# The sample block moves from the last token group to the first, and block 7 takes its seat in the dense expert pass

## The chip, the cores and the metric

One core of a Trainium2 chip. The time is the device time of one execution in microseconds (us). The kernel before took 4423.67 us, the median of three runs (4419.91 to 4437.72).

## The reference, cut to what matters

One layer is run on 1024 prompt tokens and on 64 sample tokens (8 sequences of 8). Both share all weights.

```python
n = rmsnorm(x); z = n @ w_in              # 1024 -> 7192 columns, cut into q, k, v, gates of three branches
m = sigmoid(gate_0) * (gla(...) @ w_gla_o) + sigmoid(gate_1) * (fox(...) @ w_fox_o) \
    + sigmoid(gate_2) * (mem(...) @ w_mem_o)
h = x + m @ w_out
h = h + peer(rmsnorm(h))                  # per token: 8 heads x 16 experts out of 16384
y = rmsnorm(h)
```

GLA is linear attention with a running state, FoX is causal softmax attention with forget gates, mem attends to 256 memory tokens. For a prompt token FoX looks at the tokens before it in the prompt. A sample sequence looks at 1024 cached rows through a page table, has its own GLA state and its own memory cache. PEER scores 2 x 128 keys per head, takes the best 16 pairs, and for each of the 128 chosen experts of a token forms `gelu(x . u[e]) * g * v[e]`, summed. The tables `u` and `v` have 16384 rows of 1024 floats each.

## The kernel before

Tokens are handled in nine blocks: 0 to 7 are the prompt's (128 tokens each), block 8, called SAMPLE or S, is the 64 sample tokens. `GROUPS` (L42) puts them in three groups, and `base(grp)` (L636) runs everything up to the PEER scores for a group: all weights are streamed once per group, so a group of three blocks shares each weight load. A weight product goes through `mm_w` (L256), in two ways: with a block's activations stationary (256 columns wide for each block, S too), or with the weights stationary and the tokens of the group moving (`jobs_T`, 384 or 320 columns wide: a prompt block brings 128 tokens, S brings 64). Per group there are 512 matmuls of the second kind on each of three lines (L273, L274, L277).

For a prompt block `gla` (L389), `fox_prompt` (L550) and `mem_prompt_att` (L595) run per block. Block b's FoX covers b + 1 blocks of keys. For S, `fox_sample` (L1240) fetches the cached pages with indirect DMAs that GpSimd issues (L1237), transposes and multiplies them page by page, `mem_sample` (L1363) does the same with the memory caches, and `gla_sample` (L484) carries eight states.

PEER is done in two ways. The blocks that are not in `DENSE` are gathered: `peer_gather` (L1028) fetches, for each of a token's 128 experts, the row of `u` and the row of `v` with an indirect DMA on GpSimd (L1040, L1051), and VectorE does one dot product (L1042) and one multiply-add (L1057) on each fetched row of 128 x 1024. A block is 128 such u rows and 128 v rows. The rows pass through four buffers, five in the last stage. The blocks in `DENSE` (448 tokens) are multiplied with the whole of both tables on TensorE in `peer_dense` (L1122), after the last group; this needs a table of gate weights per expert and token, `c_scr`, which `expert_weights` (L1071) writes, 16 tokens at a time (a slab): 8 slabs for a prompt block, 4 for S.

`choose` (L919) picks the experts of a block. `LATER` names blocks whose top-16 search is put off into `choose`; `HERE` names the block whose top-16 stays on chip.

The order of the instructions on each engine is fixed by a scheduler from priorities, a lower number being more urgent. `base` has the most urgent ones. `at(None, ...)` places work at half a million and up, that is behind all of `base`; the gathers run from one million upwards (`prio`), so that they fill what `base` leaves free. The functions run in program order otherwise. `peer_dense` can begin only when `base` of the last group is done, since it takes over its memory (`early.close()`). In it, `expert_weights` of the dense block of the last group comes first (L1154 to L1156), then the expert loop; the first product with the gate weights (L1194) needs the whole first piece of `c_scr` (L1178).

So before: group 0 (blocks 0, 1, 2) alone; then group 1 (3, 4, 5) with the gathers of 0, 1, 2 in the background; then group 2 (S, 6, 7), with the same background and the expert weights of 3, 4, 5; then the dense pass of 3, 4, 5, S with the gathers of 6 and 7 beside it.

Of the kernel before, what the change touches and what calls it, by code (L numbers as in the profile page):

```python
# [38 lines left out]

ROWS, ROWS2 = 4, 5  # L40
SAMPLE = 8
GROUPS = [[0, 1, 2], [3, 4, 5], [SAMPLE, 6, 7]]  # L42

DENSE = [3, 4, 5, SAMPLE]

LATER = [6, 7]

HERE = [SAMPLE]
DG, DW = 8, 9
WR = 4  # L50
CB = {"hot": 4, "stg": 1, "eg": 1}
# [3 lines left out]
def tile_hybrid(ctx: ExitStack, tc: tile.TileContext, x_prompt, x_sample, cache_fox_k, cache_fox_v,  # L55
# [23 lines left out]
    def T(tag, shape, dt=F32):  # L79
        cnt[0] += 1  # L80
        return bp.tile(shape, dt, tag=tag, name=f"{tag}_{cnt[0]}", bufs=BUFS[tag])
# [16 lines left out]
    def evac(out, in_):  # L98
        A.activation(out, in_, AF.Copy)
# [522 lines left out]
    t_scr = [dp.tile([128, 512], F32, name=f"t_scr{b}") for b in range(9)]  # L622
    s_scr = {b: dp.tile([128, 2048], F32, name=f"s_scr{b}") for b in LATER}
    e_scr = {b: dp.tile([128, 128], I32, name=f"e_scr{b}") for b in DENSE}
    g_scr = {b: dp.tile([128, 128], F32, name=f"g_scr{b}") for b in DENSE}
    c_scr = dp.tile([sum(64 if b == SAMPLE else 128 for b in DENSE) // 16, 128, 2048], F32, name="c_scr")
    q_scr = dp.tile([128, 4, 64], F32, name="q_scr")
# [8 lines left out]
    def base(grp):  # L636
# [55 lines left out]
        for half in range(2):  # L692
# [55 lines left out]
            def fin_k(b, p):  # L748
# [11 lines left out]
                evac(kT[:, :, b * 128:(b + 1) * 128], pt[:, :256].rearrange("p (j t) -> p j t", t=128))  # L760
                if b < 7 and grp is not GROUPS[-1]:
                    SP.dma_start(kT_scr[half * 256:(half + 1) * 256, b * 128:(b + 1) * 128].rearrange(
# [118 lines left out]
        for hd in range(8):  # L881
# [5 lines left out]
            for b in grp:  # L887
# [5 lines left out]
                evac(s, p2[:, :256])  # L893
                if b in LATER:
                    SP.dma_start(s_scr[b][:, hd * 256:(hd + 1) * 256], s)
                    continue
                t = last_t[:, hd * 64:(hd + 1) * 64] if b in HERE else T("tp", [128, 64])
                top16(s, t)
                if b not in HERE:
                    SP.dma_start(t_scr[b][:, hd * 64:(hd + 1) * 64], t)  # L900

    def top16(s, t):

        for j in range(2):
            x, v = s[:, j * 128:(j + 1) * 128], t[:, j * 16:(j + 1) * 16]
            i = t[:, 32 + j * 16:48 + j * 16].bitcast(U32)
            V.max(v[:, 0:8], x)
            V.max_index(i[:, 0:8], v[:, 0:8], x)
            V.match_replace(x, v[:, 0:8], x, LOWEST)
            V.max(v[:, 8:16], x)  # L910
            V.max_index(i[:, 8:16], v[:, 8:16], x)
# [7 lines left out]
    def choose(b):  # L919

        if b not in DENSE:
            eidx[b] = gp.tile([128, 128], I32, tag="ei", name=f"ei{b}", bufs=2)
            gate_w[b] = gp.tile([128, 8, 16], F32, tag="gw", name=f"gw{b}", bufs=2)
        for hf in range(2):
            hs = slice(4 * hf, 4 * hf + 4)
            w = gp.tile([128, 864], F32, tag="ch", name=f"ch{b}_{hf}", bufs=1)
            t = w[:, 0:256].rearrange("p (h c) -> p h c", h=4)
            if b in LATER:
                for hd in range(4):
                    x = w[:, 352 + hd % 2 * 256:608 + hd % 2 * 256]  # L930
                    SP.dma_start(x, s_scr[b][:, (4 * hf + hd) * 256:(4 * hf + hd + 1) * 256])
                    top16(x, w[:, hd * 64:(hd + 1) * 64])
            elif b in HERE:
                t = last_t[:, hf * 256:(hf + 1) * 256].rearrange("p (h c) -> p h c", h=4)
# [6 lines left out]
            def region(o, n):  # L941
                return w[:, o:o + 4 * n].rearrange("p (h c) -> p h c", h=4)
# [34 lines left out]
            c = slice(hf * 64, (hf + 1) * 64)  # L977
            if b in DENSE:
                ei, gw = w[:, 528:592].bitcast(I32), region(656, 16)
# [13 lines left out]
            V.tensor_tensor(gw, gw, sm[:, :, None].to_broadcast([128, 4, 16]), op=OP.mult)  # L993
            if b in DENSE:
                SP.dma_start(e_scr[b][:, c], ei)
# [126 lines left out]
    def peer_dense(ctx2, dn):  # L1122
# [6 lines left out]
        def DT(tag, shape, dt=F32):  # L1129
            cnt[0] += 1  # L1130
            return dn.tile(shape, dt, tag=tag, name=f"d{tag}_{cnt[0]}", bufs=DB[tag])

        def DP(tag):
            cnt[0] += 1
            return pd.tile([128, 512], F32, tag=tag, name=f"p{tag}_{cnt[0]}", bufs=PB[tag])
# [18 lines left out]
        for b in DENSE:  # L1154
            if b in GROUPS[-1]:
                expert_weights(b, DT, lambda: DP("c"))  # L1156
# [16 lines left out]
        for g in range(128 // DG):  # L1173
            if g * DG % 8 == 0:
                c8 = DT("c", [128, NS, 128])
                ready = NS - sum(w for b, w in zip(DENSE, widths) if b in GROUPS[-1]) // 16
                for x in (slice(0, ready), slice(ready, NS)) if g == 0 else (slice(0, NS),):
# [239 lines left out]
    M = 10 ** 6  # L1417
    urgent = [M // 2]

    def at(prio, f, *args):  # L1420

        keep, tc.cur_priority = tc.cur_priority, prio or urgent[0]
        f(*args)
        if not prio:
            urgent[0] = tc.cur_priority
        tc.cur_priority = keep


    prio = [M]

    def gather(blocks):
        for i, b in enumerate(blocks):
            prio[0] += M
            if i + 1 < len(blocks):
                at(prio[0] + M // 2, choose, blocks[i + 1])
            at(prio[0], peer_gather, b)
        prio[0] += M

    for grp in GROUPS:
        pj3[0] = grp is GROUPS[0]  # L1440
        base(grp)
        mine = [b for b in grp if b not in DENSE]
        first = [b for b in grp if b in DENSE]
        if grp is not GROUPS[-1]:
            first = mine[:1] + first
        else:
            first += mine[:1]
        for b in first:
            if b in DENSE and grp is GROUPS[-1]:
                choose(b)  # L1450
            else:
                at(None, choose, b)
            if b in DENSE and grp is not GROUPS[-1]:
                at(None, expert_weights, b)
        if mine and grp is not GROUPS[-1]:
            gather(mine)
    early.close()
# [37 lines left out]
```

## Time and profile before

| | |
|---|---|
| median of three runs | 4423.67 us |
| the profiled execution | 4433.77 us, its span 4432.0 us |
| TensorE (PE) busy | 3755.6 us, 85% |
| VectorE (DVE) busy | 3346.1 us, 75% |
| ScalarE (ACT) busy | 1796.2 us, 41% |
| GpSimd (POOL) busy | 1679.1 us, 38% |
| mean granted TensorE clock | 0.890 of full speed |

Busy times of a stretch count every moment in which the engine had an instruction in flight. PEld is the weight load of TensorE. [...] "Idle before" in a group of instructions is the time that the engine waited just before them, with what ended the wait.

### The profile page before, as it was taken

How to read it: one execution, taken by the hardware profiler on the slowest of the kernel's cores; microseconds unless marked ns; L12 is line 12 of the kernel's file. 1: busy time of each engine (PE TensorE's matmuls, PEld its weight loads, DVE VectorE, ACT ScalarE, POOL GpSimd, SP SyncE). 2: the span in 40 equal slices, each digit the busy share in tenths (PEclk: the TensorE clock that was granted, in tenths of full speed). 3: DMA queues.
4: the chain of work that ended last, by engine and by line, in shares of the span. 5: the costliest groups of instructions: out<-in, count | busy, mean ns of one | idle time of the engine just before them, and what ended most of it. 6: DMA issues, size and time to landing. Idle time of an engine off the chain costs nothing. (4 is left out here: it accounts for less than half of the span.)

```text
span 4432.0 us, 62344 instructions
## 1 busy us (share of the span) xinstructions
PE 3755.6 (85%) x21306; PEld 3288.8 (74%) x21306; DVE 3346.1 (75%) x7924; ACT 1796.2 (41%) x3637; POOL 1679.1 (38%) x1466
## 2 busy tenths in 40 slices
PE   4998998676689775787679979986999999999998
PEld 4886997564378775575556558875999899999997
DVE  3443469988788898888885457578999888888883
ACT  2555444343343333465564334444333223323332
POOL 0000003545644444534455553003445454545530
PEclk8997998787689886677689989997999999999999
DMA  3322457888899987778788899548999999999982
GB/s 110 90 84 70 131 165 227 279 274 294 277 309 332 319 267 242 260 243 273 253 277 287 307 321 320 169 140 289 329 303 339 327 332 337 341 337 327 344 297 81
DMA packets 652340, 1141.32 MB, mean 258 GB/s; under 512 B 62158, under 2 KB 445798, under 8 KB 648439
## 3 DMA queue, kind: packets, MB, share of 16 engines
q0 software_dynamic: 193616, 704.99, 45.6%
q1 hardware_dynamic: 458406, 432.35, 30.3%
q8 instruction: 169, 2.77, 0.2%
q14 instruction: 149, 1.21, 0.1%
HBM read 1073.45 MB, written 63.74 MB: 257 GB/s over the span
## 5 line engine op out<-in xcount | busy, mean ns | idle before, releaser
L1040 POOL DMA_INDIRECT u<-in_peer_u_dram,ei x640 | 783.3, 1224 | 873.2 <-DVE a L1042 347.6
L1051 POOL DMA_INDIRECT v<-in_peer_v_dram,ei x640 | 762.3, 1191 | 865.0 <-DVE acc L1057 452.6
L1042 DVE CUSTOM_DVE_ANT_0 u<-u,x 128x1024 f32<-128x1024 f32 x640 | 774.2, 1219 | 129.9 <-DMA u<-in_peer_u_dram,ei 128.3
L1057 DVE SCALAR_TENSOR_TENSOR acc<-v,a,acc 128x1024 f32<-128x1024 f32 x635 | 811.6, 1278 | 70.6 <-DMA v<-in_peer_v_dram,ei 68.2
L265 ACT ACTIVATE wh<-wr 128x512 fp32r<-128x512 f32 x568 | 354.0, 630 | 595.0 <-PE pj L274 186.2
L267 DVE TENSOR_TENSOR wl<-wr,wh 128x512 fp32r<-128x512 f32 x568 | 386.6, 685 | 219.4 <-PE pj L277 63.8
L1210 PE MATMUL py<-dwh,dvh 128*128 128x448 f32 x1024 | 373.9, 370 | 31.3 <-ACT dwh L1197 28.6
L1187 PE MATMUL pa<-xh,duh 128*128 128x448 f32 x1024 | 384.8, 376 | 1.3 <-ACT duh L1168 1.3
L1188 PE MATMUL pa<-xl,duh 128*128 128x448 f32 x1024 | 379.0, 370 | 0.0
L273 PE MATMUL pj<-aT,wh 128*128 128x384 f32 (+1 forms) x1104 | 367.3, 337 | 11.4 <-ACT X L837 4.5
L1211 PE MATMUL py<-dwl,dvh 128*128 128x448 f32 x1024 | 375.4, 367 | 1.4 <-DVE dwl L1198 1.4
L1212 PE MATMUL py<-dwh,dvl 128*128 128x448 f32 x1024 | 373.4, 368 | 0.3 <-DVE dvl L1206 0.3
L274 PE MATMUL pj<-aT,wh 128*128 128x384 f32 (+1 forms) x1104 | 362.3, 332 | 1.7 <-DVE aT L317 1.7
L281 PE MATMUL pj<-wh,aT 128*128 128x256 f32 x944 | 262.1, 301 | 30.3 <-DVE z L720 10.9
L1205 ACT ACTIVATE dvh<-dvr 128x1024 fp32r<-128x1024 f32 x128 | 134.2, 1059 | 377.2 <-PE py L1211 206.6
L282 PE MATMUL pj<-wh,aT 128*128 128x256 f32 x944 | 258.8, 297 | 2.9 <-DVE aT L847 1.5
L277 PE MATMUL pj<-aT,wl 128*128 128x384 f32 (+1 forms) x1104 | 251.8, 335 | 10.3 <-DVE wl L267 10.1
L1117 PE MATMUL cw<-hot,hot 128*128 128x128 f32 x768 | 173.9, 363 | 92.7 <-ACT stg L1118 73.8
L1190 PE MATMUL pa<-xh,dul 128*128 128x448 f32 x1024 | 240.2, 369 | 0.0
L1117 PEld LDWEIGHTS cw<-hot,hot 128*128 128x128 f32 x768 | 134.8, 248 | 138.1 <-ACT stg L1118 103.3
L1210 PEld LDWEIGHTS py<-dwh,dvh 128*128 128x128 f32 x1024 | 192.4, 189 | 48.6 <-ACT dwh L1197 28.9
L273 PEld LDWEIGHTS pj<-aT,wh 128*128 128x128 f32 x1104 | 213.1, 193 | 17.4 <-ACT X L837 6.6
(475 smaller groups left out, 8439.3 us busy)
## 6 DMA issues: line engine op xcount, KB each, us to landing
wr<-in_w_in_dram SPq DMA_DIRECT2D x168, 512.0 KB, 4.8
dvr<-in_peer_v_dram SPq DMA_DIRECT2D x128, 512.0 KB, 7.5
dur<-in_peer_u_dram SPq DMA_DIRECT2D x128, 512.0 KB, 6.6
dc<-c_scr SPq DMA_DIRECT2D x15, 1792.0 KB, 17.4
wr<-in_w_pq_dram SPq DMA_DIRECT2D x48, 512.0 KB, 4.3
c_scr<-stg SPq DMA_DIRECT2D x24, 1024.0 KB, 6.9
wr<-in_w_out_dram SPq DMA_DIRECT2D x24, 512.0 KB, 4.8
u<-in_peer_u_dram,ei POOLq DMA_INDIRECT x640, 6.2
```

What stands on the lines that cost most here:

```text
L267: V.tensor_tensor(wl, raw[:, q2:q2 + 2], wh.bitcast(F32), op=OP.subtract)
L273: PE.matmul(ps, wh[:, i, c], hi[:, k], start=k == 0, stop=False)
L274: PE.matmul(ps, wh[:, i, c], lo[:, k], start=False, stop=False)
L1040: G.indirect_dma_start(out=r, out_offset=None, in_=UR, in_offset=bass.IndirectOffsetOnAxis(ap=ei[:, s:s + 1], axis=0))
L1042: V.tensor_tensor_reduce(r, r, x2, 1.0, 0.0, OP.mult, OP.add, a[:, s:s + 1])
L1051: G.indirect_dma_start(out=r, out_offset=None, in_=VR, in_offset=bass.IndirectOffsetOnAxis(ap=ei[:, s:s + 1], axis=0))
L1057: V.scalar_tensor_tensor(acc, r, a[:, s:s + 1], acc, op0=OP.mult, op1=OP.add)
L1187: PE.matmul(pa[:, :NT], uh[:, k], xh[:, k], start=k == 0, stop=False)
L1188: PE.matmul(pa[:, :NT], uh[:, k], xl[:, k], start=False, stop=False)
L1210: PE.matmul(py[:, :NT], vh[:, j], wh, start=j == 0, stop=False)
L1211: PE.matmul(py[:, :NT], vh[:, j], wl, start=False, stop=False)
L1212: PE.matmul(py[:, :NT], vl[:, j], wh, start=False, stop=j == DG - 1)
```

## The change

The groups become (S, 0, 1), (2, 3, 4), (5, 6, 7). The dense pass takes S, 3, 4 and 7, so it has 448 tokens as before; the gathered blocks are 0, 1, 2, 5, 6. Of the last group 7 is now the dense one, and 5 and 6 are the ones with the late top-16 search. S is chosen and its expert weights are written in the background of group 1, behind everything else: a new counter `rest` gives both a priority of a hundred million and up.

```diff
-GROUPS = [[0, 1, 2], [3, 4, 5], [SAMPLE, 6, 7]]
-DENSE = [3, 4, 5, SAMPLE]
-LATER = [6, 7]
-HERE = [SAMPLE]
+GROUPS = [[SAMPLE, 0, 1], [2, 3, 4], [5, 6, 7]]
+DENSE = [SAMPLE, 3, 4, 7]
+LATER = [5, 6]
+HERE = [7]
...
     prio = [M]
+    rest = [100 * M]
...
         for b in first:
             if b in DENSE and grp is GROUPS[-1]:
                 choose(b)
-            else:
-                at(None, choose, b)
-            if b in DENSE and grp is not GROUPS[-1]:
-                at(None, expert_weights, b)
+                continue
+
+            late = b == SAMPLE
+            if late:
+                rest[0] += M
+            at(rest[0] if late else None, choose, b)
+            if b in DENSE:
+                if late:
+                    rest[0] += M
+                at(rest[0] if late else None, expert_weights, b)
```

## Rows read from the trace of the kernel before

**Rows 1.** Busy time by stretch of the span: the stretch, its length, then busy time and count of PE, PEld, DVE, ACT and POOL, the granted clock, the DMA engines' mean busy share and GB/s. The stretches are group 0, group 1, group 2 up to the sample attention, the sample attention, the rest of group 2, the entry into the dense pass, and the dense pass.

```profile
50.00:690.00 640.00, 589.88 (x3790) 545.80 (x3791) 310.69 (x894) 315.10 (x666) 15.18 (x31) 0.92 0.38 114
690.00:1590.00 900.00, 679.63 (x3860) 589.95 (x3859) 780.59 (x1952) 358.82 (x729) 450.25 (x398) 0.82 0.87 293
1590.00:2285.00 695.00, 497.54 (x2597) 398.42 (x2595) 602.82 (x1815) 361.82 (x831) 326.01 (x275) 0.72 0.78 259
2285.00:2700.00 415.00, 350.29 (x2119) 241.73 (x2120) 229.59 (x423) 172.68 (x387) 220.22 (x194) 0.92 0.87 305
2700.00:2942.00 242.00, 228.29 (x1581) 223.40 (x1580) 161.91 (x433) 106.26 (x217) 26.21 (x28) 0.97 0.59 191
2942.00:3064.00 122.00, 70.51 (x380) 61.44 (x381) 97.56 (x439) 58.79 (x138) 22.82 (x23) 0.75 0.74 256
3064.00:4376.00 1312.00, 1303.43 (x6807) 1196.66 (x6807) 1130.88 (x1880) 405.60 (x648) 611.16 (x493) 1.00 0.91 316
```

**Rows 2.** GpSimd in order of time (start, length, engine, line, operation): the first fetch of the gathers, the last step of block 2, the first fetch of block 6, the last step of block 7.

```profile
713.81 1.20 POOL L1040 DMA_INDIRECT u<-in_peer_u_dram,ei  x1 [16.67 <-DVE tp L908]
...
2767.82 0.57 POOL L1021 TENSOR_TENSOR fr<-fr,c 128x1 f32<-128x1 f32 x1
...
3005.52 1.02 POOL L1040 DMA_INDIRECT u<-in_peer_u_dram,ei  x1 [147.71 <-DVE ei L985]
...
4306.98 0.56 POOL L1021 TENSOR_TENSOR fr<-fr,c 128x1 f32<-128x1 f32 x1
```

**Rows 3.** GpSimd's busy time and count in three stretches: first the fetches of u rows (L1040), then those of v rows (L1051), then in the sample attention the fetches of cached pages (L1237); behind them the granted clock, the DMA share and GB/s.

```profile
690.00:1590.00 900.00, 230.54 (x196) 0.82 0.87 293
1590.00:2285.00 695.00, 159.95 (x124) 0.72 0.78 259
2285.00:2700.00 415.00, 75.27 (x64) 0.92 0.87 305
...
690.00:1590.00 900.00, 205.43 (x176) 0.82 0.87 293
1590.00:2285.00 695.00, 147.76 (x125) 0.72 0.78 259
2285.00:2700.00 415.00, 75.23 (x66) 0.92 0.87 305
...
2285.00:2700.00 415.00, 66.94 (x62) 0.92 0.87 305
```

**Rows 4.** TensorE's waits (engine, tile, line, what it waited for, us in total, times, longest), first in group 0 (60 to 690 us), then in group 1 (700 to 1590 us).

```profile
PE g L402 <- ACT lh L398: 12.2, 3, 4.5
...
PE g L402 <- ACT lh L398: 41.4, 4, 13.3
```

**Rows 5.** The sample attention on TensorE in 2285 to 2700 us, groups by line (count, busy us, mean ns, idle before), and TensorE's expert-weight matmuls (L1117) in that stretch.

```profile
L1305 PE MATMUL f<-PT,kv 128*64 128x128 f32 x512 | 70.5, 281 | 1.7 <-ACT PT L99 1.7
L1348 PE MATMUL po<-wr,PT 128*64 128x512 f32 x128 | 62.7, 633 | 3.2 <-DMA wr<-in_cache_fox_v_dram,c 3.2
L1300 PE MATMUL g<-c,wr 128*128 128x128 f32 x256 | 39.5, 285 | 1.1 <-DVE oT L1360 0.9 <-DMA wr<-in_cache_fox_k_dram,c 0.2
L1307 PE MATMUL f<-kv,c 64*64 64x64 f32 x256 | 28.6, 231 | 0.0
...
2285.00:2700.00 415.00, 40.41 (x220) 30.88 (x220) 0.92 0.87 305
```

**Rows 6.** TensorE's largest groups of FoX (L589, L563, L584) and of GLA (L424, L446) over the whole span.

```profile
L563 PE MATMUL f<-kv,zq 64*128 64x512 f32 (+3 forms) x192 | 100.3, 608 | 0.0
L589 PE MATMUL po<-PT,kv 128*64 128x128 f32 x576 | 91.4, 312 | 5.9 <-ACT PT L99 5.9
L424 PE MATMUL g<-c,lh 128*128 128x256 f32 (+1 forms) x272 | 61.3, 364 | 10.9 <-DVE att L447 7.8 <-ACT kE L404 3.0
L584 PE MATMUL g<-c,P 128*128 128x128 f32 x288 | 57.2, 337 | 19.4 <-ACT P L581 19.2
L446 PE MATMUL g<-XL 128*128 128x128 f32 (+1 forms) x280 | 55.4, 343 | 41.4 <-DVE XL L434 38.5 <-DVE att L447 2.3
```

**Rows 7.** One line of the weight products with moving tokens, at 384 and at 320 columns (groups by shape).

```profile
L273 PE MATMUL pj<-aT,wh 128*128 128x384 f32 x688 | 236.9, 345 | 5.8 <-ACT X L837 3.0 <-ACT tq L99 1.0 <-ACT kv L99 1.0
...
L273 PE MATMUL pj<-aT,wh 128*128 128x320 f32 x416 | 130.4, 324 | 5.6 <-ACT kv L99 2.9 <-ACT X L837 1.5 <-ACT wh L265 1.0
```

**Rows 8.** Expert weights: the matmuls of blocks 3, 4, 5 (24 slabs) over the span; ScalarE's three groups for S (4 slabs); the queue of SyncE in the entry into the dense pass (first and last store of a slab of S, then the load of the table); SyncE's waits for a block's indices (ns, min/median/max).

```profile
L1117 PE MATMUL cw<-hot,hot 128*128 128x128 f32 x768 | 173.9, 363 | 92.7 <-ACT stg L1118 73.8 <-DVE hot L1112 12.9 <-DVE a L1042 3.3
...
L1118 ACT ACTIVATE dc<-pc 128x256 f32<-128x256 f32 x32 | 18.9, 609 | 12.7 <-PE pc L1117 12.7
L1111 ACT ACTIVATE dhot<-dhot,deg 128x128 f32<-128x128 f32 x32 | 14.0, 479 | 0.0
L1110 ACT ACTIVATE dhot<-c,deg 128x128 f32<-128x128 f32 x32 | 10.6, 389 | 0.2 <-PE pc L1117 0.2
...
2993.24 0.33 SPq L1120 DMA_DIRECT2D c_scr<-dc  x1
...
3035.69 2.39 SPq L1120 DMA_DIRECT2D c_scr<-dc  x1
...
3052.30 0.99 SPq L1178 DMA_DIRECT2D dc<-c_scr  x2
...
L1086 SPq EVENT_SEMAPHORE  x3: 17/15315/21004, 1746.5 to 2217.1; - x3
```

## The prediction

> **What bounds the kernel now.** I read the time by stretch first [rows 1]. In the dense pass TensorE is busy 1303 of 1312 us at full clock: that stretch ends when its matmuls end, and they don't change (448 tokens before and after). In group 0 TensorE is busy 590 of 640 us (0.92) while GpSimd does almost nothing. In groups 1 and 2 it falls to 0.76 and 0.72 while VectorE rises to 0.87. In the sample attention TensorE is back at 0.84 and VectorE is at only 0.55.
>
> The second view is GpSimd in order of time [rows 2]. The gathers run from 714 to 2768 us, stop until 3006 us because blocks 6 and 7 aren't chosen yet, and end at 4307 us, 125 us before the span does. They are on no path that sets the end. What does set it is a chain of three: `base` of all groups (to 2942 us), the entry into the dense pass (to 3064 us), the dense pass.
>
> The gathers cost the chain something all the same, since their steps sit in VectorE's queue between steps of `base`. The waits show it: GLA's second matmul waits 12.2 us for 3 in group 0, so 4 us each, and 41.4 us for 4 beside the gathers, 10 us each [rows 4]. I price it from group 1: TensorE idles 220 us there; at group 0's idle share of 8% it would be 70. The other 150 us fall on 196 + 176 fetched rows [rows 3], 0.4 us a row.
>
> **The change, part by part**, against the profiled execution (4433.77 us, its span 4432.0). That one lies 10.1 us above the median of the runs.
>
> *Group 0 gets S for block 2.* S's four largest rows on TensorE are 201 us [rows 5]. The stretch holds 350 us of TensorE work [rows 1], 40 of it expert weights [rows 5], so S is between 201 and 310 us; I take 300, because the small groups of S, its states and `mem_sample` are in that stretch and little else. Block 2's own work goes: FoX is 249 us in three rows for 36 key blocks, 6.9 each, three of them 21 us; GLA 117 us for nine blocks, 13 us [rows 6]. The moving products fall from 384 to 320 columns, 345 to 324 ns [rows 7], on 3 x 512 matmuls: 32 us. Net 300 - 66 = 234 us of TensorE, at group 0's busy share of 0.92: **+254 us**. The first gather moves from 714 to about 968 us.
>
> *Groups 1 and 2 lose S and get one more prompt block's worth.* S goes at the 0.84 of its stretch: 300 / 0.84 = -357 us. Block 2 comes to group 1 and block 5 to group 2 in place of S. In key blocks this makes 33 in place of 30, so the same 21 us of FoX, 13 of GLA, 32 of wider products: 66 us, at 0.92 72 us before the gathers' toll. The toll: before, 621 of the 768 rows were fetched up to 2285 us [rows 3], over prompt work; 147 fell on the sample attention and the end of group 2. After, nearly all fall on prompt work: 147 x 0.4 = +59 us. Expert weights in the background fall from 24 slabs to 20 (3 and 4 with 8 each, S with 4): a slab is 174 / 24 = 7.2 us of TensorE [rows 8], four at 0.72 are -40 us. Together -357 + 72 + 59 - 40 = **-266 us**.
>
> So `base` ends about 12 us earlier. The size of S hardly matters for this, since it only changes place: it is 300 x (1/0.92 - 1/0.84) = -31 us, between +0 (it stalls in group 0 as it did) and -57 (no stall at all). The toll is what matters: between 0 and, if all of group 1's idle time is the gathers' (220 / 372 = 0.59 us a row), 87 us.
>
> *The entry into the dense pass gets 8 slabs for 4.* S's four were stored from 2993.24 to 3035.69 us, 14.2 us apart [rows 8], and the first table load with the last slab goes out at 3052.30. TensorE is busy 70 of 122 us there [rows 1]: it computes ahead for a few experts and then has no free buffer until the gate weights are in. Four more slabs are 4 x 14.2 = 57 us at that pace, 43.5 / 4 = 10.9 us each by ScalarE's work alone, 44 us [rows 8]. I take **+50 us**, 0 being the other end should the experts done ahead cover it.
>
> *At nothing:* the choice of S moves out of the entry into the background, where the choice of 7 replaces it one for one in the entry. The dense pass and its closing steps keep their counts. S's 62 page fetches leave GpSimd's queue, where they stood between the gathers (130 rows in 415 us there, 0.31 per us, against 372 in 900, 0.41 [rows 3]); this helps the gathers, which are not on the path. The added wait is SyncE's, for the indices of S at last priority: such a wait took up to 21 us [rows 8], and behind it stand weight loads for `mm_w`, whose four buffers cover a part. 0 to 21 us; I take 0.
>
> Sum: +254 - 266 + 50 = +38, so 4472 us, and 10 less against the median: 4462, rounded **4460 us**, 0.8% slower. Its own range is 4425 to 4500.
>
> [...] The granted clock was 0.92 in group 0 and in the sample attention, 0.82 and 0.72 in group 1 and the first part of group 2 [rows 1]. [...]
>
> **The rivals.**
>
> *Faster: the expert weights were on the path of group 2.* There TensorE idles 92.7 us just before their matmuls, 3.9 us a slab [rows 8]. Of the 24 slabs in group 2 only 16 stay, and S's four run in idle time of group 1 at last priority. Then 8 slabs x (7.2 / 0.72 + 3.9) = -111 us stand in place of -40, the sum is -33 us: **4391 us**. For it: no expert weights run in group 1 now, and TensorE idles 220 us there. Against it: the engines take their instructions in a fixed order, so what waits for a late VectorE step holds what is behind it. It turns the sign from the point where each of the eight slabs is worth 4.8 us more than the 5 (40 / 8) that I count; at 8.9 more it is as priced here.
>
> *Slower: the gathers become the end.* They start 254 us later, and the 238 us between 2768 and 3006 us are the cover. Blocks 5 and 6 need 1302 us as 6 and 7 did. The dense end at +38 leaves block 2 until about 3158 us, that is a pace of 768 / 2190 = 0.35 rows per us; it was 0.37 over all of 714 to 2768 and 0.36 in the first part of group 2. At 0.335, halfway to the sample stretch's 0.31, block 2 ends at 3261 us and the kernel 103 us later than forecast: **4560 us**. Against it: the 0.31 came beside S's fetches.
>
> *The change doesn't do what it says:* last priority leaves S's four slabs undone until `base` is over, four more slabs stand before the dense pass, 57 us: **4515 us**. The single buffer of `choose` (`ch`) and of the staged slab (`stg`) would hold block 2's and 3's own steps in that case.
>
> *No change:* the four added slabs hide behind experts done ahead. The sum is -12: **4412 us**.
>
> **How the numbers follow.** No change means within 0.5% of 4423.67 us (4401.6 to 4445.8), about what a measurement can tell. Forecast 0.46 (of this 0.13 falls below 4445.8, none under 4401.6), faster rival 0.30 (0.23 below 4401.6, 0.07 within), gathers 0.12, S left over 0.07, hidden slabs 0.05. Faster 0.23, same 0.13 + 0.07 + 0.05 = 0.25, slower 0.33 + 0.12 + 0.07 = 0.52. The range runs from below the faster rival to just short of the gathers' 4560: 4375 to 4545 us, leaving out about 0.1 on each side.
>
> **What would show it.** Group 0 should end near 940 us with the first fetch near 968. `base` should end within 50 us of 2942. The slabs stored in the entry should be eight, about 11 to 14 us apart, and the dense pass should start about 170 us after `base`. The gathers should have no pause, or a short one, before block 5, and end near 4310 to 4400 us. If the pace of the gathers falls under 0.35 rows per us, or the last step of the span is a gather's, the third case holds. If group 2 loses over 70 us more than its removed work, the faster one does.

## The result and the profile after

The changed kernel takes 4492.34 us, the median of four runs (4475.23 to 4497.86), beside 4430.69 us for the kernel before in the same runs: a ratio of 1.0135, with a 95% interval of 1.0097 to 1.0173. It is slower, as forecast, and it lies 32 us above the 4460 us that I gave, inside the range of 4425 to 4500. The profiled execution is the slowest of the four: 4497.86 us, with a span of 4496.0 us.

Two points cut the span: the start of the last score matmul (L890), which I take as the end of `base`, and the start of the first product with the gate weights (L1194), which ends the entry. First the two lines in the kernel before, with the stores of a block's choice (L996; count, then ns min/median/max, then first and last start):

```profile
L890 PE MATMUL f<-c,tq x288: 270/275/582, 630.6 to 2940.9; 128*128 128x128 f32 x144
...
L1194 DVE TENSOR_TENSOR dw<-dw,dc x128: 602/619/678, 3062.4 to 4367.4; 128x448 f32<-128x448 f32 x128
...
L996 SPq DMA_DIRECT2D g_scr<-ch x8: 319/326/423, 1686.3 to 2961.2; - x8
```

The same three lines of the changed kernel, and the stores of block 7's slabs in the last stage (L1120):

```profile
L890 PE MATMUL f<-c,tq x288: 269/275/583, 878.8 to 2949.9; 128*128 128x128 f32 x144
...
L1194 DVE TENSOR_TENSOR dw<-dw,dc x128: 596/618/626, 3129.9 to 4432.7; 128x448 f32<-128x448 f32 x128
...
L996 SPq DMA_DIRECT2D g_scr<-ch x8: 319/320/3873, 1111.2 to 2992.9; - x8
...
L1120 SPq DMA_DIRECT2D c_scr<-dc x8: 319/320/433, 3021.7 to 3113.4; - x8
```

`base` ends 9.0 us later, the entry grows from 121.5 to 180.0 us (+58.5), and what follows the first product is 3.4 us shorter. Together these are the 64 us between the two profiled executions.

The busy time by stretch of the changed kernel, with the columns of [rows 1]: group 0, group 1, group 2, the entry, the dense pass.

```profile
50.00:940.00 890.00, 800.83 (x5275) 666.64 (x5276) 328.57 (x974) 348.55 (x747) 84.75 (x108) 0.92 0.44 134
940.00:1840.00 900.00, 688.67 (x3858) 599.13 (x3856) 768.38 (x1962) 380.10 (x791) 427.68 (x375) 0.81 0.85 285
1840.00:2950.00 1110.00, 842.95 (x4681) 725.28 (x4681) 941.38 (x2447) 536.51 (x1181) 489.70 (x438) 0.80 0.81 274
2950.00:3130.00 180.00, 108.81 (x509) 92.44 (x508) 162.92 (x686) 98.74 (x238) 46.63 (x46) 0.66 0.77 263
3130.00:4440.00 1310.00, 1302.55 (x6810) 1200.96 (x6811) 1104.84 (x1762) 405.75 (x649) 579.38 (x476) 0.99 0.89 310
```

Group 0 keeps TensorE busy at 0.90 with S in it, and the dense pass is still TensorE's alone. In the entry VectorE is busy for 163 of its 180 us (0.91, before 0.80), and TensorE's granted clock is 0.66 (before 0.75).

GpSimd in order of time, as in [rows 2]: the first fetch, the last step of block 2, the first fetch after the pause, the last step of the last gathered block.

```profile
964.75 1.01 POOL L1040 DMA_INDIRECT u<-in_peer_u_dram,ei  x1 [24.64 <-DVE zt L909]
...
2968.64 0.56 POOL L1021 TENSOR_TENSOR fr<-fr,c 128x1 f32<-128x1 f32 x1
...
3033.90 1.01 POOL L1040 DMA_INDIRECT u<-in_peer_u_dram,ei  x1 [64.70 <-DVE ei L985]
...
4326.59 0.56 POOL L1021 TENSOR_TENSOR fr<-fr,c 128x1 f32<-128x1 f32 x1
```

The pace over blocks 0 to 2 is 768 rows in 2004 us, 0.38 a us. The pause has shrunk to 65 us but is still there, and the last gather ends 144 us before the last matmul of the dense pass starts (4470.6 us).

The queue of SyncE in the entry of the changed kernel shows what the dense pass waits for: eight slab stores, and the last table load only behind them. The first two columns are start and length in us; xN is the number of issues joined in a row.

```profile
3021.68 0.33 SPq L1120 DMA_DIRECT2D c_scr<-dc  x1
3036.07 0.43 SPq L1120 DMA_DIRECT2D c_scr<-dc  x1
3046.06 22.79 SPq L1120 DMA_DIRECT2D c_scr<-dc  x3
3082.12 15.94 SPq L1120 DMA_DIRECT2D c_scr<-dc  x2
3104.22 0.37 SPq L1178 DMA_DIRECT2D dc<-c_scr  x1
3113.43 0.32 SPq L1120 DMA_DIRECT2D c_scr<-dc  x1
3123.12 1.00 SPq L1178 DMA_DIRECT2D dc<-c_scr  x2
```

From first to last store it is 91.7 us for seven intervals, 13.1 us each; S's four took 42.5 us for three [rows 8]. TensorE works ahead on the first products of the expert loop, one piece of 128 experts at a time (called an expert here, as in the prediction). It does six of these ahead in both kernels, and in the changed one the last of them is under way at 3022.1 us, when only the first slab is stored (L1187 in the entry, first and last start):

```profile
L1187 PE MATMUL pa<-xh,duh x48: 359/367/721, 2984.6 to 3022.1; 128*128 128x448 f32 x48
```

### The profile page after: what moved, and what is told of

Read it like the earlier page. It is cut to its first block, busy times and chain, and to the rows that moved or that the text cites. A ratio compares the mean times of both kernels' runs of the same rounds, so it can differ in the third digit from the quotient of the medians.

```text
span 4496.0 us, 62331 instructions
## 1 busy us (share of the span) xinstructions
PE 3779.6 (84%) x21306; PEld 3315.4 (74%) x21306; DVE 3338.6 (74%) x7924; ACT 1786.5 (40%) x3630; POOL 1635.3 (36%) x1466
## 5 line engine op out<-in xcount | busy, mean ns | idle before, releaser
L1040 POOL DMA_INDIRECT u<-in_peer_u_dram,ei x640 | 765.0, 1195 | 888.9 <-DVE a L1042 427.5
L1051 POOL DMA_INDIRECT v<-in_peer_v_dram,ei x640 | 749.1, 1170 | 912.3 <-DVE acc L1057 429.7
L273 PE MATMUL pj<-aT,wh 128*128 128x384 f32 (+1 forms) x1104 | 374.1, 342 | 16.8 <-ACT tq L99 5.6
L1187 PE MATMUL pa<-xh,duh 128*128 128x448 f32 x1024 | 382.5, 374 | 0.0
L274 PE MATMUL pj<-aT,wh 128*128 128x384 f32 (+1 forms) x1104 | 368.4, 336 | 0.0
L273 PEld LDWEIGHTS pj<-aT,wh 128*128 128x128 f32 x1104 | 213.7, 194 | 22.9 <-ACT tq L99 6.9
L281 PEld LDWEIGHTS pj<-wh,aT 128*128 128x128 f32 x944 | 194.2, 207 | 37.3 <-DVE z L720 10.2
L274 PEld LDWEIGHTS pj<-aT,wh 128*128 128x128 f32 x1104 | 213.7, 194 | 0.4 <-DVE aT L317 0.4
```

The lines of the kernel that those rows point to most:

```text
L273: PE.matmul(ps, wh[:, i, c], hi[:, k], start=k == 0, stop=False)
L274: PE.matmul(ps, wh[:, i, c], lo[:, k], start=False, stop=False)
L281: PE.matmul(ps, hi[:, k, :], wh[:, i], start=k == 0 and first, stop=False)
L1040: G.indirect_dma_start(out=r, out_offset=None, in_=UR, in_offset=bass.IndirectOffsetOnAxis(ap=ei[:, s:s + 1], axis=0))
L1051: G.indirect_dma_start(out=r, out_offset=None, in_=VR, in_offset=bass.IndirectOffsetOnAxis(ap=ei[:, s:s + 1], axis=0))
L1187: PE.matmul(pa[:, :NT], uh[:, k], xh[:, k], start=k == 0, stop=False)
```

## The experiments

**Four slabs in place of eight.** In the changed kernel the entry computes only four of block 7's eight slabs and stores each of them twice.

```diff
-        for sb in range(w // 16):
+        half = H is not H_base
+        for sb in range(4 if half else w // 16):
...
+            if half:
+                SP.dma_start(c_scr[o + sb + 4], stg.rearrange("p n t -> p (n t)"))
```

> The changed kernel, but at the entry into the dense pass only four of block 7's eight slabs are computed, and each is stored twice (so the gate weights of 64 tokens of block 7 are those of the other 64). Theory (the four added slabs are serial, 13.1 us each in the trace of the changed kernel): about 50 us less, 4440 us, base unchanged, the entry (last score matmul to first product with the gate weights) 180 us to about 128. Rival (the entry is longer because VectorE and SyncE come late to it, and the slabs fit beside that): 10 to 20 us less, 4475 us.

Measured: 4436.42 us, 1.0025 of the kernel before (1.0010 to 1.0041), 56 us under the changed kernel, and 45 us under its later median of 4481.24 us (below). The entry, from the last score matmul to the first gate product, in the columns of [rows 1]:

```profile
2933.00:3068.80 135.80, 73.44 (x382) 64.27 (x380) 110.41 (x510) 60.25 (x139) 23.93 (x23) 0.72 0.75 260
```

135.8 us in place of 180.0 (forecast: about 128). All the rest of the change is in this kernel, and what is left of the loss is 12 us. The four slabs are most of it.

**Eight slabs in place of four.** The other way round: in the kernel before, each of S's four slabs is computed and stored twice.

```diff
-        for sb in range(w // 16):
+        for sb in sorted(list(range(w // 16)) * (1 if H is H_base else 2)):
```

> The kernel before, but each of S's four slabs at the entry into the dense pass is computed and stored twice, the second time over the first. Theory (slabs are serial): 44 to 57 us more than before, about 4480 us, nearly all of the change's loss without any change of the groups. Rival: TensorE works ahead on experts behind them, under 20 us more, 4445 us.

Measured: 4472.7 us, 1.0092 (1.0064 to 1.0119), 48 us more than the kernel before. The entry:

```profile
2952.20:3124.30 172.10, 106.42 (x510) 91.69 (x508) 151.61 (x637) 95.75 (x234) 52.88 (x45) 0.66 0.78 270
```

Four more slabs lengthen the entry by 50.6 us with the old grouping too, at the same granted clock of 0.66. So the price comes with the slabs and not with the new order around them, and little or none of it hides behind the experts done ahead.

**Few early gathers, old and new grouping.** To see `base` without its toll, blocks 0 to 2 gather one head of eight (96 rows in place of 768) in each kernel; the edit is the same in both.

```diff
+HEADS = {0: 1, 1: 1, 2: 1}
...
+        nh = HEADS.get(b, 8)
...
-        for hd in range(8):
-            if hd < 7:
+        for hd in range(nh):
+            if hd < nh - 1:
```

> The kernel before, with one of eight heads of the gathers of blocks 0, 1 and 2 kept (96 of 768 rows; the other experts of these blocks are left out). Toll of 0.4 us a row for rows over prompt work, next to none over the sample attention: base (to the last score matmul, 2941 us before) ends about 220 us earlier, near 2720 us. Rival (the gathers cost base nothing, VectorE's own steps do): within 50 us of 2941.

> The changed kernel with the same cut. Toll of 0.4 us a row, all rows over prompt work: base (2950 us) ends about 270 us earlier, near 2680 us, so some 40 us before that of the kernel before with the same cut; the choice of block 7 comes 20 us after the end of base in place of 43, because no gather of block 2 is left then. Rival (the toll is the same in both kernels): base ends 10 us later than that of the kernel before with the same cut.

Measured: `base` ends at 2508.1 us with the old grouping and at 2472.2 us with the new one, 36 us earlier (the kernels take 4006.31 and 4016.33 us, one run each). The difference is as expected (some 40 us), but `base` ends 433 and 478 us earlier than with all gathers, where 220 and 270 were expected: the toll of all rows is nearly double my price. The choice of block 7 is stored 21.1 us after `base`, as expected. From the first fetch to the end of `base`, the old grouping with all gathers and then, in a fence of its own, with few:

```profile
714.00:2941.00 2227.00, 1737.43 (x10061) 1437.47 (x10059) 1749.91 (x4484) 989.47 (x2141) 1021.02 (x890) 0.83 0.82 275
```

```profile
714.00:2508.00 1794.00, 1590.38 (x10059) 1346.94 (x10058) 976.75 (x3453) 925.28 (x2083) 198.41 (x218) 0.91 0.46 145
```

The same for the new grouping, with all gathers and with few:

```profile
965.00:2950.00 1985.00, 1511.89 (x8436) 1306.40 (x8434) 1684.75 (x4270) 905.33 (x1949) 917.02 (x811) 0.81 0.83 281
```

```profile
965.00:2472.00 1507.00, 1340.44 (x8432) 1201.73 (x8431) 935.90 (x3294) 846.33 (x1896) 126.33 (x145) 0.92 0.44 139
```

These four lines answer what a gathered row costs. TensorE has the same matmuls with and without the 672 rows (x10061 and x10059). Its idle time falls by 286 us, from 490 to 204, and its busy time by 147 us, with the granted clock rising from 0.83 to 0.91. So a row costs 0.43 us of idle time and 0.22 us of slower matmuls, 0.64 us in all; in the new grouping the two are 307 and 171 us, 0.71 us a row. These are means over all rows, those beside the sample attention included.

**S at ordinary priority.** In the changed kernel, S's choice and expert weights get the priority that blocks 3 and 4 have.

```diff
-            late = b == SAMPLE
+            late = False
```

> The changed kernel with the choice and the expert weights of S at the same priority as those of blocks 3 and 4 (before the gathers instead of behind them). Theory (S's four slabs hide in group 1 either way): within 10 us of the changed kernel, 4482 to 4502 us. Rival (the last priority is what keeps the new order from losing more): the first gather starts later or base ends later, 4510 us or more. Other rival (S at last priority holds buffers that blocks 2 and 3 need): 4470 us or less.

Measured: 4467.88 us, 1.0107 (1.0076 to 1.0137), 24 us under the changed kernel, which was measured in other runs. By its number this is the rival that has S's late steps hold buffers, at 4470 us or less. `base` ends at 2910.4 us and the entry is 181.5 us, as long as before the edit.

**The collision at the end of `base`.** Block 2's last gather (2968.64 us) now falls into the entry, and block 7's choice is stored 43.0 us after `base` (2992.9 - 2949.9), where S's was stored after 20.3 (2961.2 by L996 of the kernel before). To test that, block 2 gathers six heads of eight.

```diff
+HEADS = {2: 6}
```

> The changed kernel with six of eight heads in the gather of block 2 alone (64 rows left out). By the cut of the other runs a row costs base 0.71 us, so base ends some 45 us earlier, near 2905 us. Theory of the collision (block 2's gather now ends 19 us after base, and its last steps and loads stand before the choice of block 7 on VectorE and before the dense loads on SyncE): the choice of block 7 is stored 20 us after base in place of 43. Rival (the choice is late for another reason): still about 43 us.

Measured in a single run: 4458.17 us, with `base` ending at 2913.2 us. The choice is stored 21.7 us after `base`, so it was the collision that made it late. But the entry is 180.2 us, as in the changed kernel, with the slabs now 15.0 us apart (2969.4 to 3074.1 us):

```profile
2913.20:3093.40 180.20, 106.01 (x510) 91.39 (x508) 157.42 (x645) 97.45 (x236) 53.61 (x49) 0.65 0.76 264
```

VectorE is again busy for 0.87 of the entry. What the choice gains, the slabs lose. With S at ordinary priority it is the other way round: the choice is stored 54.0 us after `base`, the slabs are 11.8 us apart, VectorE is busy for 0.90, and the entry is as long again:

```profile
2910.40:3091.90 181.50, 104.98 (x510) 89.56 (x508) 164.25 (x661) 99.94 (x240) 49.42 (x49) 0.69 0.77 267
```

So the entry as a whole was steadier than the pace of its slabs. The next block's gathers begin earlier in the run with six heads, 65 us after `base` in place of 84; that their steps on VectorE are the cause is an inference.

**More experts ahead.** Six buffers in place of four for the products that wait for the gate weights let TensorE work further ahead during the slabs; room for them is taken from the buffers in which the slabs' operands are built. The edit is the same in both kernels.

```diff
-"w": 4, ... "hot": 7
+"w": 6, ... "hot": 4
```

> The kernel before with six buffers in place of four for the products that wait for the gate weights (and four in place of seven for the staging of the expert weights, to make room). In all runs TensorE does exactly six experts ahead in the entry; now it could do eight, 2 x 24 matmuls of 0.2 us, 10 us off the dense pass: 4415 us. Rival (smaller staging slows the slabs as much): 4425 us or more.

> The changed kernel with the same edit: 10 us less, 4480 us, if the experts ahead count; with the rival 4490 us or more. In neither case does it come under the kernel before.

Measured: 4449.0 us with the old grouping (1.0043, 1.0026 to 1.0059) and 4513.89 us with the new one (1.0205, 1.0179 to 1.0231), both slower, so the forecast of 10 us less failed, and the numbers are the rival's. TensorE does eight experts ahead in place of six, as meant, but the slabs slow to 22.5 and 19.4 us each, and the entries grow to 140.5 and 227.8 us. The stores of the slabs in the entry, with the old grouping and then with the new one:

```profile
L1120 SPq DMA_DIRECT2D c_scr<-dc x4: 319/323/327, 2996.7 to 3064.2; - x4
```

```profile
L1120 SPq DMA_DIRECT2D c_scr<-dc x8: 319/320/327, 3004.3 to 3139.8; - x8
```

What follows the first gate product is 0.3 us shorter with the old grouping and 9.6 us with the new one. Over the other profiled kernels with all gathers, this part differs by 14.5 us, so what the two more experts buy is not settled. The edit changes two things at once, and no run has the smaller buffers alone. Together they cost more than they give.

**The changed kernel again, and S's priority again.** The changed kernel unaltered, and beside it, on the same chip, the edit of its priority from above.

> The changed kernel once more, unaltered, beside the next run on the same chip, for two questions. First, how far base moves from run to run with one and the same order: base ended at 2949.9 us in the first profile and at 2933.0 and 2927.6 us in two kernels with the same order up to the entry. If the 9 us by which base came later in the first profile were the spread of runs, this one ends base between 2925 and 2950 us and takes 4470 to 4490 us; if they belong to the change, base ends within 5 us of 2950 and the kernel takes 4490 us or more. The entry is 175 to 185 us long by both.

> The changed kernel with S's choice and expert weights at ordinary background priority, once more, on the same chip as the run before it. Theory that the last priority costs something, because S's steps then hold buffers and queue places late in group 1: 15 to 30 us less than the unaltered kernel, base ends near 2910 us. Rival, that the 24 us seen between two calls were the spread of runs: within 8 us of the unaltered kernel in the median. The entry stays at 180 us by both, so neither brings it below the kernel before.

Measured: the changed kernel 4481.24 us (1.0133, 1.0111 to 1.0155), with S at ordinary priority 4477.19 us (1.0118, 1.0098 to 1.0138). The end of `base` in the repeated profile of the changed kernel:

```profile
L890 PE MATMUL f<-c,tq x288: 270/275/582, 882.4 to 2935.9; 128*128 128x128 f32 x144
```

This is 14 us earlier than in the first profile with one and the same program, so the 9 us by which `base` came later lie within the spread of runs. The order on each engine is the same up to the entry in the kernels with four slabs and with six buffers: with theirs, the new grouping has four ends of `base`, 2949.9, 2935.9, 2933.0 and 2927.6 us, mean 2936.6. The old grouping has three, 2940.9, 2952.2 and 2940.4 us, mean 2944.5. The new one is 8 us earlier in the mean, which is within the spread of these few profiles.

On S's priority the two comparisons don't agree: 24 us, then 4 us side by side, where the theory wanted 15 to 30 and the rival under 8. Over all ten runs of each, the means are 4486.4 and 4474.8 us, 11.6 apart with standard errors of 2.7 and 2.5, so some 4 to 19 us. In its two profiles `base` ends at 2910.4 and 2913.9 us, before all four ends above, so the order of S's steps does reach `base`; but what follows the first gate product is 1376 and 1373 us long, against 1368 and 1367 in the changed kernel, and takes back a part of it, though no more than this part differs between runs. The last priority probably costs a little; how much, and through which buffer or queue, stays open. It isn't the loss: without it the kernel is still slower than before.

No version that does all the work ran faster than the kernel before. The nearest with the new grouping ran at 1.0107 (S at ordinary priority), and even with four slabs left out it ran at 1.0025.

## Why the prediction was right, and where its sizes were off

**The terms.** The repeated profile (4480.97 us) is at its kernel's median, so it stands beside the first. All against the profiled kernel before.

| term | forecast | first profile | repeated profile |
|---|---|---|---|
| group 0, by the first fetch | +254 | +250.9 | +255.0 |
| groups 1 and 2 | -266 | -241.9 | -260.0 |
| `base` in all | -12 | +9.0 | -5.0 |
| entry | +50 | +58.5 | +56.1 |
| dense pass and closing steps | 0 | -3.4 | -3.9 |
| sum | +38 | +64 | +47 |

The mechanism held in the main: S changes its place for nearly nothing, and the loss is four more slabs between `base` and the dense pass.

**Group 0** came out within 4 us, by two errors that cancel. Over stretches that differ by 250 us (50 to 690 in [rows 1], 50 to 940 after) TensorE's busy time grows by 211 us, from 589.88 to 800.83, where I had 234; S is smaller than the 300 us that I took, 277 us if the 66 us for block 2 are right. But its share sinks to 0.90, where I kept 0.92. 211 us more work at that worse share gives the same 250.

**Groups 1 and 2** were too low a sum by 6 to 24 us, and the step that failed is the toll of a gathered row, 0.4 us. The idle time that I worked it out from was right: the runs with few gathers show 0.43 us a row. What I left out is that the same matmuls run longer beside the gathers, 147 us over 672 rows, which makes 0.64 us (0.71 in the new grouping). I had seen the granted clock of 0.72 to 0.82 in [rows 1] and priced it at zero, taking the busy shares to hold some of it. They can't: a busy share counts a slow matmul as work. With few gathers idle time and clock recover together (490 to 204 us, 0.83 to 0.91); no run here takes the one away without the other, so what lowers the clock is not shown. Busy time times granted clock is nearly the same with and without the rows, 1442 and 1447 us, as it would be if the clock alone made the matmuls longer; as the granted clock is a mean over idle time too (0.50 from 3112 to 3130 us of the changed kernel, where TensorE is busy for 0.8 of 18 us), this is an argument and not a proof.

That the total was close all the same is in part luck: one error made up for another. I priced S and the four slabs at busy shares that held toll already (0.84 and 0.72), and then added a toll for the 147 rows. At group 0's 0.92 the terms without gathers are 254 - 326 + 72 - 31 = -31 us, and the pair with few gathers shows -36. My net toll was then the other 19 of the -12, and the runs show 28, the difference between -36 and the mean of -8. This rests on a single run of each kernel with few gathers, and on ends of `base` that spread over some 20 us, so neither the 28 nor its 9 us over my 19 is firm.

GLA's waits, by which I had shown the toll, stay as they were: some 4 us each without gathers, 11 us with them. In the changed kernel, group 0 and then group 1, as in [rows 4]:

```profile
PE g L402 <- ACT lh L398: 8.9, 2, 4.5
...
PE g L402 <- ACT lh L398: 44.7, 4, 14.8
```

**The entry** was forecast at +50, between 44 and 57, and is +56 to +58.5, at the upper end and just over it. Seven intervals of 13.1 us are nearer to S's 14.2 us than to the 10.9 us of ScalarE's work alone. The four slabs added 49.3 us between first and last store; the choice came 22.7 us later by the collision with block 2, of which the steps behind it gave back 13.4 (3.2 before the first slab, 10.2 after the last). I did not foresee the collision, and the run with six heads shows that its removal doesn't shorten the entry.

What sets the 13 us was not isolated. From the first slab's store to the last, VectorE is the busiest engine, 85 of 90 us:

```profile
3022.00:3112.00 90.00, 60.10 (x250) 50.22 (x249) 85.17 (x298) 64.73 (x166) 34.41 (x33) 0.60 0.83 293
```

Of VectorE's 163 us in the entry, 45 are the slabs' own steps (22 in the kernel before) and 51 the dot products and multiply-adds of the gathers (22 before). That the slabs' pace holds only beside these gathers is a rival that no run takes away: each kernel here has gathers in its entry.

**At nothing.** The dense pass kept its length. S at last priority, which I took at 0 with 21 us as its other end, costs some 4 to 19 us by the runs with ordinary priority; that it is SyncE's wait for S's indices that costs them wasn't shown.

**From profile to median.** I took 10 us off because the profiled execution before lay above its median. The changed kernel's first profile lay 5.5 us above its own median and the repeated one on it. Against the repeated median of 4481.24 us the forecast is 21 us low (32 against the first one, 4492.34): 9 of these are the terms above, 10 this step, and 2 my rounding.

**The rivals.** The faster one fell: groups 1 and 2 became 242 to 260 us shorter, where it needed 337 (-266 with -111 in place of -40). With few gathers the new grouping gains 36 us in `base`, about what its plain terms give. The gathers did not become the end: their pace was 0.38 rows per us, over the 0.35 from which it would have turned. S was not left over: all 20 slabs of S, 3 and 4 were stored before the entry, the last at 2627.5 us. That the added slabs hide was excluded from both sides, by four slabs fewer (45 to 56 us less) and four more (48 us more). The pair with few gathers agrees: its entries are 126.9 and 172.6 us, 46 apart.

## What to carry to other kernels

Count the work that stands alone between two stages, at the pace that it has there, before looking at how the stages trade: here some 250 us moved for nearly nothing, and four slabs of 13 us decided. The toll of background work on TensorE was idle time and longer matmuls here, 286 and 147 us; read both, by the same instruction count with and without it. Compare ends of stages over several profiles of one order before reading ten microseconds as an effect.

## What the runs showed of the hardware that was not expected

The same 128x128 matmul of the slabs (L1117) slowed within the longer entry. In the kernel before, and then in the changed one, over the entry:

```profile
L1117 PE MATMUL pc<-dhot,dhot x128: 270/275/582, 2977.0 to 3034.6; 128*128 128x128 f32 x128
```

```profile
L1117 PE MATMUL pc<-dhot,dhot x256: 270/421/583, 3005.0 to 3112.3; 128*128 128x128 f32 x128
```

The median goes from 275 to 421 ns between the same extremes, with the granted clock at 0.66 in place of 0.75. The experts ahead are nearly done at 3022 us. Up to then, from 2984 us, the granted clock is 0.98 and TensorE is busy for all of the 38 us; after that it has little but these (222 of 250 matmuls, with 29.6 us of waits before them) and is granted 0.60 (the stretch 3022 to 3112 us above). The slabs are no slower for it (13.1 us against 14.2 in the kernel before); but there they share TensorE with the experts ahead, so this doesn't show that the clock has no part in their pace.

Idle time and longer matmuls together made the toll of a fetched row half as large again as the idle time alone, 0.64 us against 0.43. And one fixed order of instructions up to the end of `base` ended it between 2927.6 and 2949.9 us in four profiles, a spread of 22 us.
